# Two-operand work moved from GpSimd to VectorE, and an experts' activation taken by one ScalarE function from PSUM

## The chip, the cores and the metric

The kernel runs on one core of a Trainium2 chip. The core has TensorE (PE in the profile: matmuls, with weight loads listed as PEld), VectorE (DVE), ScalarE (ACT), GpSimd (POOL) and SyncE (SP), which here only issues transfers; 16 DMA engines move data. The metric is device microseconds (us) of one execution, lower is better. Everything is computed in f32 or better: a matrix product is made of three matmuls on a high and a low part of each operand (`hi` = the rounded operand, `lo` = operand − `hi`), so that for each tile loaded from memory somebody has to compute a copy `hi` and a difference `lo`.

## What is computed

Two layers run on 512 tokens of width 1024 (an mLSTM with dilated attention, then differential attention with RWKV). The end of the last layer, and the only place that the change touches, is a feed-forward part with 16384 experts of which each token uses 8 heads x 16:

```
q    = (xc @ peer_wq).reshape(C, 8, 2, 128)
s    = einsum('chpd,hpkd->chpk', q, peer_keys)
sv, si = top_k(s, 16)
cand = sv[..., 0, :, None] + sv[..., 1, None, :]
top_s, pos = top_k(cand.reshape(C, 8, 256), 16)
eidx = 128 * si[..., 0, a] + si[..., 1, b]          # a, b from pos
gate = softmax(top_s)
act  = gelu(einsum('chkd,cd->chk', peer_u[eidx], xc))
out  = einsum('chk,chkd->cd', gate * act, peer_v[eidx])
```

## The kernel before

`peer` (lines 2205 to 2417) does that part, after some 3100 us of the other layers. The 512 tokens are four blocks of 128. The first three (ND = 3) go a dense way: u·h is computed for all 128 blocks of 128 experts, each result multiplied by a dense gate matrix that is zero where a token did not choose an expert, and v is summed over all blocks. The fourth block fetches its chosen rows of u and v by indirect transfers on GpSimd (`gathered`).

**Routing.** Four steps g = 0 to 3 project the tokens with a quarter of `peer_wq` each. `wtile` (line 250) loads a 128x512 piece, ScalarE copies `whi`, and line 259 computes `wlo`, in turn on VectorE and GpSimd as long as `wboth` is true and on GpSimd alone afterwards (it goes false after the first half of g = 0). `route` takes the top 16s on VectorE (lines 2421 to 2425), and `experts` (after g = 1 and 3) turns positions into expert numbers: line 2476 compares (`eq`, VectorE), line 2477 multiplies by `sf` (GpSimd), line 2480 sums (VectorE).

**Building the gate matrix.** `gate_matrix` does 16 groups of 8 tokens for each of the three token blocks. A group makes four one-hot tiles of 128x1024 f16 from `iota` and the transposed numbers `tr`: `hot[0]`, `hot[1]` by comparing (lines 2521, 2522), `hot[2]`, `hot[3]` by multiplying `hot[0]` (lines 2523, 2524); `hot[3]` goes to GpSimd in every other group. 16 matmuls (line 2529 on) multiply the one-hots into the PSUM banks `acc0` to `acc3`, ScalarE copies each bank into `stage`, and each 32 tokens SP writes a `stage` to the table `wg` in DRAM (line 2536).

**Early blocks.** Between these, `early` (line 2279) computes u·h for NA = 34 of the 128 expert blocks, woven in by fixed counts (A0 = 40 steps before the building, AE = 24 in each token block, the rest behind): load a 128x1024 row block `raw` (line 2274), copy `uh` (ScalarE, line 2277), difference `ul` (line 2278, on GpSimd), 24 matmuls (lines 264 to 266), a copy `x` from PSUM (ScalarE, line 2293); six of the `x` stay, the others go to DRAM (`xd`). The first loads, copies and differences of these blocks carry a raised priority (HE), so the scheduler issues them well ahead, with three buffers of `uh`, `ul`. The scheduler (Tile) sets each engine's order from its own estimates; each engine then works strictly in that order and waits by semaphores.

**The main loop** (`for i in range(-7, P)`, written out in its order by `Core`, whose operations all carry line 62) does one expert block per iteration, with stages of several iterations at once: load v (512 KB), from i = 29 on also u (512 KB) and its 24 matmuls; the slice of the gate table, `W`, each fourth iteration; the activation of block i + 4 and i + 3; its product with `W` (`x<-x,W`); the parts `ah` (ScalarE) and `al` (VectorE) of that product; the parts of v (`v<-raw,v` on VectorE); and 18 matmuls of 512 columns into `acc`. The activation is the tanh form of gelu in four operations on 128x384 f32: Square (ScalarE), `gq<-gq,x` (VectorE), Tanh (ScalarE), `x<-gq,x` (VectorE), less a factor 0.5 that sits in the scale of the gate matrix. Up to i = 38 each iteration also takes one step of the fourth block's route on VectorE, afterwards its gathered rows.

Of the kernel before, what the change touches and what calls it, by code (L numbers as in the profile page):

```python
# [10 lines left out]
F32 = mybir.dt.float32  # L11
# [4 lines left out]
AF = mybir.ActivationFunctionType  # L16
ALU = mybir.AluOpType
AX = mybir.AxisListType
PSUM = bass.MemoryType.PSUM
P = 128  # L20
# [188 lines left out]
class Net:  # L209
# [40 lines left out]
    def wtile(self, w, r0, c0, n):  # L250

        nc = self.nc
        raw = self.wraw.tile([P, T], F32, tag="wraw", name=self.uid("wraw"))
        nc.sync.dma_start(raw[:, :n], w[r0:r0 + P, c0:c0 + n])
        hi = self.wsp.tile([P, T], F32R, tag="whi", name=self.uid("whi"))
        lo = self.wsp.tile([P, T], F32R, tag="wlo", name=self.uid("wlo"))
        nc.scalar.copy(hi[:, :n], raw[:, :n])
        self.wodd = not self.wodd
        (nc.vector if self.wodd and self.wboth else nc.gpsimd).tensor_tensor(lo[:, :n], raw[:, :n], hi[:, :n].bitcast(F32), op=ALU.subtract)
        return hi, lo  # L260

    def mm3(self, ps, lh, ll, rh, rl, first, last):
# [1942 lines left out]
    def peer(self, out):  # L2205

        nc, tc, a, c = self.nc, self.tc, self.a, self.c
        ND = NT - 1
        with ExitStack() as st:
# [71 lines left out]
            def early():  # L2281

                for i in [*range(NK, NA), *range(NK)]:
                    with tc.high_priority(HE):
                        uh, ul = split(a["ut"][i], "u", nc.gpsimd)
                    ps = ups.tile([P, T], F32, tag="u", name=self.uid("u"))[:, :n]
                    for k in range(KD):
                        b = slice(k * P, (k + 1) * P)
                        self.mm3(ps, uh[:, b], ul[:, b], hh[:, k, :n], hl[:, k, :n], k == 0, k == KD - 1)
                        if k % 2 and k < KD - 1:  # L2290
                            yield
                    x = xt()
                    nc.scalar.copy(x, ps)
                    if i < NK:
                        q["x", i] = x
                    else:
                        nc.sync.dma_start(xd[i], x)
                    yield
# [35 lines left out]
            for i in range(-7, P):  # L2334
# [22 lines left out]

                g = i + 3
                if 0 <= g < P:
                    x, h = q["x", g], q.pop(("h", g))  # L2360
                    k.scalar.activation(h, h, AF.Tanh, scale=0.044715 * math.sqrt(2.0 / math.pi))
                    k.vector.scalar_tensor_tensor(x, h, 1.0, x, op0=ALU.add, op1=ALU.mult)
                    k.vector.tensor_tensor(x, x, q["W", g // 4 * 4][:, :, g % 4], op=ALU.mult)
                g = i + 4
                if 0 <= g < P:
                    if g >= NA:
                        q["x", g] = xt()
                        k.scalar.copy(q["x", g], q.pop(("ps", g)))
                    x, h = q["x", g], gt("gq")
                    q["h", g] = h  # L2370
                    k.scalar.activation(h, x, AF.Square)
                    k.vector.scalar_tensor_tensor(h, h, 1.0 / 0.044715, x, op0=ALU.add, op1=ALU.mult)
                if 0 <= i + 1 < P:
                    x = q.pop(("x", i + 1))
                    ah, al = q["a", i + 1] = gt("ah", 2, F32R), gt("al", 2, F32R)
# [81 lines left out]
    def experts(self, g, dst, rt, nc):  # L2457
# [16 lines left out]
        for j, x in enumerate((a, b)):  # L2474
            eq = eqs[j] = rt.tile(sh, F16, tag="eq", name=self.uid("eq"), bufs=2)
            nc.vector.tensor_tensor(eq, x[:, :, None, :].to_broadcast(sh), self.i16[:, None].to_broadcast(sh), op=ALU.is_equal)
            nc.gpsimd.tensor_tensor(eq, eq, sf[:, j:8:2, :, None].to_broadcast(sh), op=ALU.mult)
        for j, eq in eqs.items():
            yield
            nc.vector.tensor_reduce(out=dst[1 + j][:, 2 * g - 2:2 * g + 2], in_=eq.rearrange("p h j k -> p h k j"), op=ALU.add, axis=AX.X)  # L2480
# [16 lines left out]
    def gate_matrix(self, t, gate, part, wg, bank, bp, iota):  # L2497
# [14 lines left out]
        for c0 in range(0, P, CH):  # L2512
            stage = bp.tile([P, P // 4, CH, 4], F32, tag="stage", name=self.uid("stage"), bufs=2)
            for q in range(0, CH, B):
# [6 lines left out]
                nc.vector.tensor_tensor(hot[0], iota[:, None].to_broadcast(sh), bc(0), op=ALU.is_equal)  # L2521
                nc.vector.tensor_tensor(hot[1], iota[:, None].to_broadcast(sh), bc(1), op=ALU.is_equal)  # L2522
                nc.vector.tensor_tensor(hot[2], hot[0], bc(2), op=ALU.mult)  # L2523
                (nc.gpsimd if n.start % 16 else nc.vector).tensor_tensor(hot[3], hot[0], bc(3), op=ALU.mult)  # L2524
                for e in range(B):
                    if e % 4 == 0:
                        ps = bank(f"acc{n.start // 4 % 2 * 2 + e // 4}")
# [2 lines left out]
                    nc.tensor.matmul(o, of(1, e), of(3, e), start=False, stop=True)  # L2530
                    if e % 4 == 3:
                        nc.scalar.activation(stage[:, :, q + e - 3:q + e + 1].rearrange("p g t e -> p t g e"),
                                             ps.rearrange("p (t g e) -> p t g e", t=4, e=4), AF.Copy, scale=0.5 / 1024)
                yield
            n = t * P + c0
            nc.sync.dma_start(wg[:, :, n:n + CH].rearrange("g j t e -> j g (t e)"), stage.rearrange("p g t e -> p g (t e)"))

    def gelu(self, x, tl, out=None):

        nc = self.nc  # L2540
        q = tl(list(x.shape), "gq")
        nc.scalar.activation(q, x, AF.Square)
        nc.vector.scalar_tensor_tensor(q, q, 1.0 / 0.044715, x, op0=ALU.add, op1=ALU.mult)
        nc.scalar.activation(q, q, AF.Tanh, scale=0.044715 * math.sqrt(2.0 / math.pi))
        out = q if out is None else out
        nc.vector.scalar_tensor_tensor(out, q, 1.0, x, op0=ALU.add, op1=ALU.mult)
        return out

    def gathered(self, t, h, gate, ei, out, gp, m5, row, Xd):

# [32 lines left out]
                yield  # L2583
        while held:
            step(None, None, dot)
        q = self.gelu(act, tl)
        nc.vector.scalar_tensor_tensor(q, q, 0.5, gate, op0=ALU.mult, op1=ALU.mult)
        yield
        for k in range(P):
            step(a["peer_v_2"][0], k, add)  # L2590
# [65 lines left out]
```

## Time and profile before

| | us |
|---|---|
| three runs | 4447.52, 4453.7, 4455.69 |
| median | 4453.7 |
| profiled execution, its own time | 4451.97 |
| its span in the profile | 4450.2 |

| engine | busy us | share of the span |
|---|---|---|
| TensorE | 4139.1 | 93% |
| VectorE | 3076.5 | 69% |
| ScalarE | 1979.0 | 44% |
| GpSimd | 1698.1 | 38% |

The shares are means over stages with different limits. For the change only the last 1350 us matter, and they are read by stage: the routing (3100 to 3263 us), the building of the gate matrix (3263, the first one-hot, to 3446, the last), the hand-over to the main loop (to 3482.5, its first matmul into `acc`), the loop's iterations without u matmuls (i = 0 to 28, to 3633.6), those with them (to 4402), and the tail. A duration in the profile is one instruction's; where instructions of an engine overlap slightly, the distance from start to start is what one costs.

### The profile page before, as it was taken

The page shows a single profiled execution, that of the slowest core. Times are in us where ns is not written, and L with a number is a line of the kernel's source. Part 1 is how long each engine was busy: PE and PEld are TensorE (multiplying, and loading weights), DVE is VectorE, ACT ScalarE, POOL GpSimd, SP SyncE. Part 2 cuts the span into 40 slices and gives each one's busy share as a digit, 9 for nine tenths or more (in the row PEclk, how much of TensorE's full clock was granted, in tenths as well). Part 3 has the DMA queues.
Part 4 walks back from the last instruction along what each step waited for, and adds up shares of the span by engine and source line. Part 5 has one row for each costly group of instructions (what it writes and reads, how often), then busy time and mean ns, then how long its engine had stood idle before and what let it go on. Part 6 is the DMA issues. An engine that isn't in the chain of part 4 may idle for free. (4 is left out here: it accounts for less than half of the span.)

```text
span 4450.2 us, 83415 instructions
## 1 busy us (share of the span) xinstructions
PE 4139.1 (93%) x32239; PEld 3601.2 (81%) x32239; DVE 3076.5 (69%) x5903; ACT 1979.0 (44%) x4240; POOL 1698.1 (38%) x1501
## 2 busy tenths in 40 slices
PE   7999999899999899989999999998877889999998
PEld 6889998788888788767777777777767779999997
DVE  4665224565565665546776676646999797999999
ACT  3544234355323445435555555534234444444443
POOL 3324444333444343322333333425355102445443
PEclk8999999899999999989999999999988999999999
DMA  4325334333556421110000001265256657999997
GB/s 138 79 58 164 93 96 129 88 77 97 162 173 201 132 75 55 49 33 20 29 29 26 29 27 42 75 194 186 71 164 196 197 173 269 339 348 338 334 339 258
DMA packets 437062, 621.08 MB, mean 140 GB/s; under 512 B 32868, under 2 KB 318708, under 8 KB 436536
## 3 DMA queue, kind: packets, MB, share of 16 engines
q1 hardware_dynamic: 393464, 472.17, 33.8%
q0 software_dynamic: 36864, 134.23, 8.5%
q10 hardware_dynamic: 6336, 9.35, 0.7%
q8 instruction: 253, 4.15, 0.4%
q14 instruction: 145, 1.19, 0.1%
HBM read 549.36 MB, written 48.24 MB: 134 GB/s over the span
## 5 line engine op out<-in xcount | busy, mean ns | idle before, releaser
L62 POOL TENSOR_TENSOR wlo<-wraw,whi 128x512 fp32r<-128x512 f32 x451 | 613.5, 1367 | 883.9 <-ACT whi L62 840.7
L62 ACT CAST whi<-wraw 128x512 fp32r<-128x512 f32 x572 | 347.4, 617 | 555.2 <-PE mm L62 369.1
L62 PE MATMUL acc<-v,ah 128*128 128x512 f32 x1536 | 417.7, 394 | 4.3 <-ACT ah L62 4.3
L62 PE MATMUL u<-hph,u 128*128 128x384 f32 x1504 | 398.8, 336 | 0.0
L62 PE MATMUL mm<-whi,u 128*128 128x256 f32 x2048 | 376.8, 285 | 4.9 <-ACT u L62 1.9
L62 PE MATMUL mm<-xh,whi 128*128 128x512 f32 (+2 forms) x880 | 341.2, 388 | 8.1 <-ACT r L62 5.1
L1497 POOL TENSOR_TENSOR wbl<-wblk,wbh 128x256 fp32r<-128x256 f32 (+1 forms) x184 | 149.4, 812 | 510.8 <-ACT wbh L1496 349.5
L62 PEld LDWEIGHTS acc<-v,ah 128*128 128x128 f32 x1536 | 291.5, 191 | 60.0 <-ACT ah L62 4.6
L62 PEld LDWEIGHTS mm<-whi,u 128*128 128x128 f32 x2048 | 323.0, 193 | 6.9 <-ACT u L62 2.5
L62 PE MATMUL mm<-xh,wlo 128*128 128x512 f32 (+2 forms) x880 | 328.0, 373 | 0.0
L62 PE MATMUL mm<-xl,whi 128*128 128x512 f32 (+2 forms) x880 | 328.0, 373 | 0.0
L62 PE MATMUL mm<-wlo,u 128*128 128x256 f32 x1024 | 291.5, 285 | 5.1 <-POOL wlo L62 4.6
L62 PEld LDWEIGHTS u<-hph,u 128*128 128x128 f32 x1504 | 273.1, 188 | 3.7
L62 PE MATMUL acc<-v,al 128*128 128x512 f32 x768 | 242.7, 398 | 28.7 <-DVE al L62 28.6
L2557 POOL DMA_INDIRECT gr<-in_peer_u_dram,ei x128 | 165.1, 1290 | 251.6 <-DVE act L2571 158.3
L62 PE MATMUL u<-hpl,u 128*128 128x384 f32 x752 | 252.7, 336 | 0.0
L2557 POOL DMA_INDIRECT gr<-in_peer_v_dram,ei x128 | 170.0, 1328 | 183.4 <-DVE pr L2578 152.8
L62 PE MATMUL mm<-whi,xh 128*128 128x256 f32 x768 | 237.5, 309 | 0.0
L62 PE MATMUL mm<-whi,xl 128*128 128x256 f32 x768 | 220.7, 287 | 1.0 <-POOL xl L62 1.0
L62 PE MATMUL mm<-wlo,xh 128*128 128x256 f32 x768 | 220.2, 287 | 0.0
L62 DVE TENSOR_TENSOR wlo<-wraw,whi 128x512 fp32r<-128x512 f32 x121 | 102.5, 847 | 147.2 <-ACT whi L62 141.5
L62 PEld LDWEIGHTS mm<-wlo,u 128*128 128x128 f32 x1024 | 197.7, 193 | 6.6 <-POOL wlo L62 5.4
(598 smaller groups left out, 11734.3 us busy)
## 6 DMA issues: line engine op xcount, KB each, us to landing
raw<-in_ut_dram SPq DMA_DIRECT2D x128, 512.0 KB
raw<-in_peer_v_dram SPq DMA_DIRECT2D x128, 512.0 KB
wraw<-in_w_in_dram SPq DMA_DIRECT2D x184, 256.0 KB
wraw<-in_w_down_dram SPq DMA_DIRECT2D x160, 256.0 KB
wraw<-in_w_up_dram SPq DMA_DIRECT2D x152, 256.0 KB
mraw<-in_w_mod_dram SPq DMA_DIRECT2D x96, 256.0 KB
wg<-stage SPq DMA_DIRECT2D x12, 2048.0 KB
W<-wg SPq DMA_DIRECT2D x32, 768.0 KB
```

Of the source, the lines that this page charges most:

```text
L62: return lambda *a, **k: self.tc.keep_in_program_order(f(*a, **k))
L1497: (nc.vector if self.wn > WN and n % 2 else nc.gpsimd).tensor_tensor(lo, raw, hi.bitcast(F32), op=ALU.subtract)
L2557: tc.keep_in_program_order(nc.gpsimd.indirect_dma_start(out=r, out_offset=None, in_=w, in_offset=bass.IndirectOffsetOnAxis(ap=ei[:, i:i + ...
```

## The change

Three things change.

1. The differences and products that GpSimd did in `peer` with two operand tiles go to VectorE: `wlo` at line 259 once `wboth` is false, `ul` of the early blocks (line 2278), the product of `eq` with `sf` (line 2477), and `hot[3]` (line 2524). GpSimd keeps the indirect transfers.
2. The activation becomes one ScalarE instruction, the tanh-form gelu function, and reads PSUM in the place of the copy that was there: in `early` the `x` that is stored is already activated; in the loop Square, Tanh and the two VectorE operations are gone, and for blocks from 34 on the copy from PSUM is the activation. The function includes the factor 0.5, so the gate matrix is scaled by 1/1024 and not by 0.5/1024.
3. The gathered block's activation is one function too, and one product on VectorE in place of three operations.

```diff
-        (nc.vector if self.wodd and self.wboth else nc.gpsimd).tensor_tensor(lo[:, :n], ...)
+        (nc.vector if self.wodd or not self.wboth else nc.gpsimd).tensor_tensor(lo[:, :n], ...)
...
-                        uh, ul = split(a["ut"][i], "u", nc.gpsimd)
+                        uh, ul = split(a["ut"][i], "u", nc.vector)
...
-                    nc.scalar.copy(x, ps)
+                    nc.scalar.activation(x, ps, AF.Gelu_apprx_tanh)
...
-                    x, h = q["x", g], q.pop(("h", g))
-                    k.scalar.activation(h, h, AF.Tanh, scale=0.044715 * math.sqrt(2.0 / math.pi))
-                    k.vector.scalar_tensor_tensor(x, h, 1.0, x, op0=ALU.add, op1=ALU.mult)
+                    x = q["x", g]
                     k.vector.tensor_tensor(x, x, q["W", g // 4 * 4][:, :, g % 4], op=ALU.mult)
...
-                        k.scalar.copy(q["x", g], q.pop(("ps", g)))
-                    x, h = q["x", g], gt("gq")
-                    q["h", g] = h
-                    k.scalar.activation(h, x, AF.Square)
-                    k.vector.scalar_tensor_tensor(h, h, 1.0 / 0.044715, x, op0=ALU.add, op1=ALU.mult)
+                        k.scalar.activation(q["x", g], q.pop(("ps", g)), AF.Gelu_apprx_tanh)
...
-            nc.gpsimd.tensor_tensor(eq, eq, sf[:, j:8:2, :, None].to_broadcast(sh), op=ALU.mult)
+            nc.vector.tensor_tensor(eq, eq, sf[:, j:8:2, :, None].to_broadcast(sh), op=ALU.mult)
...
-                (nc.gpsimd if n.start % 16 else nc.vector).tensor_tensor(hot[3], hot[0], bc(3), op=ALU.mult)
+                nc.vector.tensor_tensor(hot[3], hot[0], bc(3), op=ALU.mult)
...
-                                             ps.rearrange("p (t g e) -> p t g e", t=4, e=4), AF.Copy, scale=0.5 / 1024)
+                                             ps.rearrange("p (t g e) -> p t g e", t=4, e=4), AF.Copy, scale=1.0 / 1024)
...
-        q = self.gelu(act, tl)
-        nc.vector.scalar_tensor_tensor(q, q, 0.5, gate, op0=ALU.mult, op1=ALU.mult)
+        q = tl([P, P], "gq")
+        nc.scalar.activation(q, act, AF.Gelu_apprx_tanh)
+        nc.vector.tensor_tensor(q, q, gate, op=ALU.mult)
```

Everything up to the routing stays as it was. From there on the scheduler orders anew, and the lines of `gate_matrix` and `experts` are numbered six lower. The functions of the activation and of the softmax's exponential do not lie in one table of ScalarE: nine table loads are added, seven of them before the loop (between line 2485, the exponential, and line 2293) and two in the loop at i = 38.

VectorE while the gate matrix is built, before. `hot_N<-iota` are the comparisons, `hot_N<-hot_M` the products, `tr` belongs to a token block:

```order
L2521 TENSOR_TENSOR hot_41828<-iota_40510,tr_41004 128x1024
L2521 TENSOR_TENSOR hot_41865<-iota_40510,tr_41004 128x1024
L2522 TENSOR_TENSOR hot_41829<-iota_40510,tr_41004 128x1024
L2523 TENSOR_TENSOR hot_41830<-hot_41828,tr_41004 128x1024
L2524 TENSOR_TENSOR hot_41831<-hot_41828,tr_41004 128x1024
L2521 TENSOR_TENSOR hot_41914<-iota_40510,tr_41004 128x1024
L2521 TENSOR_TENSOR hot_41948<-iota_40510,tr_41004 128x1024
L2522 TENSOR_TENSOR hot_41866<-iota_40510,tr_41004 128x1024
L2523 TENSOR_TENSOR hot_41867<-hot_41865,tr_41004 128x1024
```

The same place on VectorE after the change:

```order
L2515 TENSOR_TENSOR hot_41702<-iota_40510,tr_40926 128x1024
L2516 TENSOR_TENSOR hot_41703<-iota_40510,tr_40926 128x1024
L2517 TENSOR_TENSOR hot_41704<-hot_41702,tr_40926 128x1024
L2518 TENSOR_TENSOR hot_41705<-hot_41702,tr_40926 128x1024
L2278 TENSOR_TENSOR u_41988<-raw_41985,u_41987 128x1024
L2515 TENSOR_TENSOR hot_41747<-iota_40510,tr_41004 128x1024
```

Every group has its four one-hots on VectorE, and the difference of an early block stands in the same queue behind every second or third group.

VectorE at the end of the routing's step g = 2, before (`iota` is the building's table, `cd` and `ts` are the second top 16):

```order
L2446 TENSOR_TENSOR cd_40293<-sv_40270 128x2x16
L2449 TENSOR_TENSOR cd_40293<-sv_40270 128x2x24
L2443 CAST sf_40268<-si_40271 128x64
L2449 TENSOR_TENSOR cd_40293<-sv_40270 128x2x48
L2302 CAST iota_40510<-tables_39092 128x256
L2421 MAX ts_39105<-cd_40293 128x8 x2
```

The same place after:

```order
L2417 MATCH_REPLACE cd_40293<-ts_39105,cd_40293 128x88 x2
L2418 MAX ts_39105<-cd_40293 128x8 x2
L2419 MAX_INDEX ps_40269<-ts_39105,cd_40293 128x8 x2
L2278 TENSOR_TENSOR u_40685<-raw_40682,u_40684 128x1024
L259 TENSOR_TENSOR wlo_40423<-wraw_40420,whi_40422 128x512
L259 TENSOR_TENSOR wlo_40441<-wraw_40438,whi_40440 128x512
L2278 TENSOR_TENSOR u_40719<-raw_40716,u_40718 128x1024
L2302 CAST iota_40510<-tables_39092 128x256
L2415 MAX sv_40852<-S_40307 128x8
```

The last two `wlo` of the projection g = 3 now stand behind the whole route of g = 2, and right ahead of the route of g = 3 (`S_40307`), which reads that projection.

VectorE in the loop's iterations without u matmuls, before:

```order
L62 SCALAR_TENSOR_TENSOR gq_43629<-gq_43629,x_43533 128x384
L62 TENSOR_TENSOR al_43633<-x_43410,ah_43632 128x384
L62 TENSOR_TENSOR v_43637<-raw_43531,v_43636 128x1024
L62 MAX sv_43615<-S_39098 128x8
L62 MAX_INDEX si_43616<-sv_43615,S_39098 128x8
L62 MATCH_REPLACE S_39098<-sv_43615,S_39098 128x128
L62 MAX sv_43615<-S_39098 128x8
L62 MAX_INDEX si_43616<-sv_43615,S_39098 128x8
L62 SCALAR_TENSOR_TENSOR x_43533<-gq_43629,x_43533 128x384
L62 TENSOR_TENSOR x_43533<-x_43533,W_43408 128x384
```

The same place after:

```order
L62 TENSOR_TENSOR x_43454<-x_43454,W_43380 128x384
L62 TENSOR_TENSOR al_43575<-x_43382,ah_43574 128x384
L62 TENSOR_TENSOR v_43579<-raw_43488,v_43578 128x1024
L62 MAX sv_43562<-S_39098 128x8
L62 MAX_INDEX si_43563<-sv_43562,S_39098 128x8
L62 MATCH_REPLACE S_39098<-sv_43562,S_39098 128x128
L62 MAX sv_43562<-S_39098 128x8
L62 MAX_INDEX si_43563<-sv_43562,S_39098 128x8
L62 TENSOR_TENSOR x_43490<-x_43490,W_43380 128x384
```

The two SCALAR_TENSOR_TENSOR of an iteration are gone, and nothing else of it has moved.

## Rows read from the trace of the kernel before

**Rows 1.** Busy time by stage; columns: us, then PE, PEld, DVE, ACT, POOL, PEclk, DMA, GB/s:

```profile
3100.00:3263.00 163.00, 132.96 (x698) 119.76 (x697) 156.45 (x708) 46.67 (x98) 77.10 (x46) 0.91 0.29 90
3263.00:3446.30 183.30, 139.54 (x1148) 125.80 (x1148) 180.42 (x171) 75.09 (x134) 105.68 (x42) 0.89 0.64 194
3446.30:3482.50 36.20, 31.88 (x203) 31.24 (x201) 5.74 (x9) 15.18 (x27) 12.02 (x5) 0.97 0.70 227
3482.50:3633.60 151.10, 130.32 (x522) 100.37 (x523) 146.64 (x365) 69.42 (x119) 5.24 (x2) 0.96 0.55 173
3633.60:4402.00 768.40, 768.21 (x3913) 702.40 (x3912) 735.82 (x956) 357.64 (x559) 332.32 (x252) 1.00 0.90 322
```

**Rows 2.** Timeline of VectorE in the building; columns: start, duration, operation:

```profile
3423.93 2.86 DVE L2523 TENSOR_TENSOR hot<-hot,tr 128x1024 f16<-128x1024 f16 x1
...
3429.62 0.68 DVE L2523 TENSOR_TENSOR hot<-hot,tr 128x1024 f16<-128x1024 f16 x1
3430.22 0.68 DVE L2522 TENSOR_TENSOR hot<-iota,tr 128x1024 f16<-128x1024 f16 x1
```

**Rows 3.** Timeline of GpSimd in the same stretch; in brackets its idle time before:

```profile
3423.64 2.60 POOL L2278 TENSOR_TENSOR u<-raw,u 128x1024 fp32r<-128x1024 f32 x1 [1.50 <-ACT u L2277]
...
3435.01 1.98 POOL L2524 TENSOR_TENSOR hot<-hot,tr 128x1024 f16<-128x1024 f16 x1 [6.47 <-PE acc L2530]
```

**Rows 4.** Groups of GpSimd, 3100 to 3482 us: busy, mean ns | idle before, releaser:

```profile
L2278 POOL TENSOR_TENSOR u<-raw,u 128x1024 fp32r<-128x1024 f32 x34 | 87.1, 2568 | 66.7 <-ACT u L2277 66.6
L2524 POOL TENSOR_TENSOR hot<-hot,tr 128x1024 f16<-128x1024 f16 x24 | 57.8, 2410 | 51.2 <-PE acc L2530 31.1 <-DVE hot L2521 20.1
L259 POOL TENSOR_TENSOR wlo<-wraw,whi 128x512 fp32r<-128x512 f32 x22 | 28.1, 1296 | 19.0 <-ACT whi L257 19.0
L2477 POOL TENSOR_TENSOR eq<-eq,sf 128x1024 f16<-128x1024 f16 x12 | 23.0, 1916 | 41.8 <-DVE pb L2469 32.2 <-DVE eq L2476 9.6
```

**Rows 5.** Stage of the building, instructions on `hot` alone; columns: us, PE, PEld, DVE, POOL:

```profile
3263.00:3446.30 183.30, 57.93 (x736) 47.13 (x736) 177.90 (x168) 57.84 (x24) 0.89 0.64 194
```

**Rows 6.** Groups of VectorE, 3100 to 3482 us:

```profile
L2470 DVE TENSOR_SCALAR pz<-pa 128x64 f32<-128x64 f16 x6 | 11.6, 1936 | 0.0
L2443 DVE CAST sf<-si 128x64 f16<-128x64 uint32 x12 | 6.7, 557 | 0.0
...
L2467 DVE SCALAR_TENSOR_TENSOR pb<-pa,ps 128x64 f16<-128x64 f16 x6 | 1.3, 213 | 0.0
```

**Rows 7.** VectorE's differences, tiles `u` and `wlo`: ns least/median/most, first and last start:

```profile
L62 DVE TENSOR_TENSOR u<-raw,u x94: 1206/1217/1232, 3631.5 to 4397.6; 128x1024 fp32r<-128x1024 f32 x94
...
L259 DVE TENSOR_TENSOR wlo<-wraw,whi x6: 674/680/1381, 3053.9 to 3071.7; 128x512 fp32r<-128x512 f32 x6
```

**Rows 8.** Timeline of VectorE in an iteration of the loop's first stage:

```profile
3501.01 0.54 DVE L62 SCALAR_TENSOR_TENSOR x<-gq,x 128x384 f32<-128x384 f32 x1
3501.58 0.85 DVE L62 TENSOR_TENSOR x<-x,W 128x384 f32<-128x384 f32 x1
3502.34 0.56 DVE L62 SCALAR_TENSOR_TENSOR gq<-gq,x 128x384 f32<-128x384 f32 x1
3502.81 0.56 DVE L62 TENSOR_TENSOR al<-x,ah 128x384 fp32r<-128x384 f32 x1
```

**Rows 9.** Pieces of the chain that ended last: start, duration, instructions:

```profile
3650.94 4.17 PE u L62 x24
3655.11 4.08 PE acc L62 x18
```

**Rows 10.** Timeline of SP's queue at the hand-over:

```profile
3451.76 0.37 SPq L2536 DMA_DIRECT2D wg<-stage  x1
...
3461.27 0.79 SPq L2344 DMA_DIRECT2D W<-wg  x2
```

**Rows 11.** Timeline of PE in the tail:

```profile
4419.52 0.73 PE L62 MATMUL acc<-v,al 128*128 128x512 f32 x2 [2.87 <-DVE al L62]
```

**Rows 12.** ScalarE's table loads in the whole kernel: busy, mean ns | idle before:

```profile
L62 ACT ACT_TABLE_LOAD x4 | 5.1, 1283 | 0.1
```

More of the change, by code (lines that the diff above doesn't have):

```diff
@@ L258, in wtile @@
         self.wodd = not self.wodd
-        (nc.vector if self.wodd and self.wboth else nc.gpsimd).tensor_tensor(lo[:, :n], raw[:, :n], hi[:, :n].bitcast(F32), op=ALU.subtract)
+        (nc.vector if self.wodd or not self.wboth else nc.gpsimd).tensor_tensor(lo[:, :n], raw[:, :n], hi[:, :n].bitcast(F32), op=ALU.subtract)
         return hi, lo
@@ L2536, in gate_matrix @@
             nc.sync.dma_start(wg[:, :, n:n + CH].rearrange("g j t e -> j g (t e)"), stage.rearrange("p g t e -> p g (t e)"))
[L2538 to L2547, printed above, removed]
     def gathered(self, t, h, gate, ei, out, gp, m5, row, Xd):
```

## The prediction

> **What bounds the kernel now.** I read the busy time by stage first, because the change touches only what lies behind 3100 us [rows 1]. In the building VectorE is busy 180.4 of 183.3 us, TensorE 139.5; in the loop's first stage VectorE 146.6 of 151.1, TensorE 130.3; then, with u matmuls, TensorE 768.2 of 768.4. So VectorE is the bound up to 3633.6 us, but for the hand-over, and TensorE from there on. Whatever the change gives must come from the first three stages and the tail; the stage of 768 us can give nothing.
>
> Next, why VectorE is full in the building. Its timeline beside GpSimd's is what to see: a one-hot that took 2.86 us began at 3423.93, while GpSimd computed a two-operand difference from 3423.64 to 3426.24; at 3429.62 the same operation took 0.68 us, and the next began 0.60 later [rows 2]. GpSimd had nothing then: its instruction at 3435.01 has 6.47 us of idle time before it, back to 3428.5 [rows 3]. So VectorE waits inside its instruction until GpSimd's ends. The whole stage says the same: 168 one-hots take 177.9 us, 1.06 each [rows 5], against 0.60 undisturbed.
>
> **Part 1, the building: what it removes.** Four kinds of GpSimd instruction leave: 34 differences of u, 24 one-hots, 22 `wlo`, 12 products, 196.0 us together [rows 4]. With them the blocking goes. The 168 one-hots at 0.60 would be 100.8, so 77.1 less [rows 2, 5]. `pz` at 1.936 us and `sf` at 0.557 are small operations beside one of the same shape at 0.213; 6 x 1.72 = 10.3 and 12 x 0.34 = 4.1 [rows 6]. That is 91.5 us off VectorE.
>
> **What it adds.** All of it to VectorE's queue: 34 differences of u at 1.22, the loop's own price for that operation, 41.5; 22 `wlo` at 0.68, 15.0 [rows 7]; 24 one-hots and 12 products of the same size and type at 0.60, 14.4 and 7.2 [rows 2]. Together 78.1. Net VectorE gains 91.5 - 78.1 = 13.4 us between 3100 us and the last one-hot.
>
> In detail it moves the load between stages: routing gets all `wlo` and products and, by the order, some ten of the u differences, and grows; the building then has 192 one-hots at 0.60 (115) and some 24 differences (29), 144 us in place of 180, close to TensorE's 139.5. There two things can eat into the gain. The order puts the last two `wlo` of the projection g = 3 behind the whole route of g = 2, so the scores that the next route reads come later; at the worst VectorE idles while the 24 matmuls of 512 columns that read these two run (18 such take 4.08 [rows 9], so 5.4) and the scores are copied: by estimate up to 7 us. And each u difference now waits in VectorE's queue for ScalarE's copy, with one-hots behind it. On the other side smaller operations that I didn't price (`pb`, `ei`, `cd`) also lose their blocking. I set these against each other and keep 13.4, with 0 to 35 as bounds.
>
> The upper bound is TensorE itself: 139.5 + 31.9 of the 219.5 us up to the first matmul into `acc`.
>
> **Table loads.** Nine are added; one takes 1.283 us [rows 12], 11.5 together, on an engine busy 75 of 183 us [rows 1]. Three pairs lie at exponentials while VectorE still routes other token blocks; only the last can delay the first one-hot, by 2.6 at most. I take 0. The Trainium skill, "ScalarE: Activation LUTs", section What ACT_TABLE_LOAD costs, adds a drain and gives about 2.66 us per switch; by that the nine would be 24 us and the bound for the last pair 5.3, still beside VectorE's work. The trace has the load's 1.283 and shows no drain.
>
> **Part 2, the hand-over.** From the last one-hot to the first matmul into `acc` 36.2 us pass [rows 1]. Two things end late there. SP writes the last `stage` at 3451.76 and fetches the first `W` at 3461.27 [rows 10], and the product and its split must follow; and TensorE still has 6.5 early blocks at 4.17 [rows 9] to do, 27 us. By the new order 2.75 of them stand behind the last one-hot, 11.5 us. The write and fetch remain: 5.5 from the last one-hot to the write, 9.5 to the fetch, and by estimate some 9 for the transfer and the product. 36.2 becomes about 24: 12 less, with bounds 0 and 17. These early blocks go to where TensorE had gaps, in the building, which is the cover; if TensorE gets behind there, this gain goes back.
>
> **Part 3, the loop without u matmuls.** An iteration loses two VectorE operations. From start to start `x<-gq,x` costs 0.57 and `gq` 0.47 [rows 8], 1.04 together, 30.2 in 29 iterations. VectorE falls from 146.6 to 116.4. TensorE becomes next: 18 matmuls are 4.08 [rows 9], 29 x 4.08 = 118.3. The two are as good as equal, so some waiting remains; I take the floor and the 4.5 us that VectorE idled before: 123, 28 less. Bounds: 33 (the floor) and 15 (half, if transfers or the chain over `ah` and `al` set the pace; the DMA engines are at 0.55 here against 0.90 in the next stage, which speaks against it). ScalarE loses two operations and a copy's place is taken by the function; at 69 of 151 us its price doesn't matter.
>
> **Part 4, the rest.** From 3633.6 on an iteration is 4.17 + 4.08 on TensorE: 0. VectorE, at 735.8 of 768.4 us, is nearly late there, and is late in the tail: TensorE waits four times for `al`, 0.83 to 2.87 us, 7.7 together; the longest is shown [rows 11]. With 1.04 us less per iteration VectorE has slack, and I take 7 of it, bounds 3 and 8. The gathered block's activation is one instruction once: nothing.
>
> **Sum.** 13.4 + 12 + 28 + 7 = 60.4 us. The profiled execution took 4451.97, so 4391.6; the median of the runs lies 1.7 higher, 4393.3. I predict 4393.
>
> **Rivals.**
> *The building doesn't get shorter (4419).* VectorE gains 36 us there, but TensorE, its matmuls interleaved with one-hots by fixed counts, is at a granted clock of 0.89 and hardly below VectorE's new load; routing grows by as much as the building shrinks, or the late scores take it. Then only loop and tail count, 28 + 7: 4418.7. For it: 144 against 139.5. Against: the hand-over's blocks have to be done some time, and TensorE had 44 us of gaps.
> *TensorE-bound throughout (4365).* VectorE's waits vanish: 219.5 - 171.4 = 48 up to `acc`, 33 in the loop, 8 in the tail, 89 together: 4365. For it: the unpriced small operations, and the blocking of 91.5 all gone. Against: 139.5 is the sum, and one-hots and matmuls must alternate.
> *Slower: the waits go into VectorE's queue (4479).* GpSimd's queue stood waiting for ScalarE's copies 66.6 us before u differences and 19.0 before `wlo` [rows 4]. On an idle engine that costs nothing. In VectorE's queue each such wait holds up the one-hots behind it, and through them the matmuls and the `stage`. All 85.6 us of it would end at 4453.7 - 60.4 + 85.6 = 4479; from 60.4 of 85.6, some 70%, the change loses. For it: the order shows each u difference straight ahead of one-hots. Against: the loads and copies have raised priority and three buffers, and ScalarE is at 41% in the building, so most of the waits were of an engine ahead of its need.
> *The change doesn't do it (4485).* If the one-hots stay at 1.06 us because something other than GpSimd slows them, 91.5 us of the sum are missing: 4453.7 + 31.1 = 4485. Against: the pairs of rows at 3423.9 and 3429.6.
> The Trainium skill, "Perfetto Trace Analysis", section Optimizing Scalar/DVE Operations, speaks for this side: with a saturated VectorE it suggests to move work to ScalarE or even GpSimd, the reverse of this change, and by that alone the 78.1 us would be added where VectorE is full. The same passage warns that the two share a read port, so that moving between them may not help; rows 2 and 3 agree with the warning, 2.86 against 0.68 us.
>
> **How the numbers follow.** Chances: the forecast, 4375 to 4410, 0.63; building unchanged 0.16; TensorE-bound 0.10; waits in VectorE's queue 0.08 (0.03 of it so partial that nothing is measured); no effect on the one-hots 0.03. The range 4362 to 4430 takes in the forecast and the two cases beside it. Below 0.2%, about 9 us, a measurement of this kernel can't tell a difference from none. Faster: 0.63 + 0.16 + 0.10 = 0.89; same 0.03; slower 0.08.
>
> **What would show it.** One-hots of 0.68 us throughout, and VectorE near 145 us in a building of about 150; routing longer than 163; the loop's first stage near 123 with TensorE above 95%; the stage from i = 29 at 768; no waits for `al` in the tail. I am wrong where VectorE's rows before a u difference or a `wlo` show idle time released by ScalarE, where one-hots keep durations above 1 us, or where the first `W` product waits on a late `wg` as long as now.

## The result, and the profile after

The changed kernel takes 4370.19 us (median of four runs, 4367.73 to 4373.44) against 4451.76 of the kernel before (four runs, 4447.52 to 4455.69): a ratio of 0.9821, with a 95% interval of 0.9809 to 0.9833. That is 81.6 us less where 60.4 were forecast; 4393 was predicted, in a range from 4362 to 4430. The direction, the places and the mechanism held; three of the four terms were too small and the fourth a little too large, and the largest miss is in the building. The time lies in the range, but below the band of 4375 to 4410 to which the forecast itself gave a chance of 0.63.

The profiled execution took 4373.44 us, 78.5 less than that of before. Its busy time by stage, cut at the same events as [rows 1]: the first and the last one-hot, the first matmul into `acc`, the first u matmul, and close to the last one. Columns: us, then PE, PEld, DVE, ACT, POOL, granted clock, DMA share, GB/s.

```profile
3100.00:3254.00 154.00, 137.80 (x743) 123.88 (x742) 142.46 (x653) 54.49 (x105) 0.00 (x0) 0.97 0.33 101
3254.00:3423.20 169.20, 141.98 (x1234) 124.79 (x1233) 166.97 (x327) 83.79 (x145) 0.00 (x0) 0.91 0.72 226
3423.20:3441.50 18.30, 12.90 (x84) 12.42 (x83) 2.69 (x3) 5.03 (x10) 0.00 (x0) 0.91 0.77 244
3441.50:3566.50 125.00, 123.04 (x522) 99.22 (x523) 119.80 (x319) 46.48 (x62) 0.00 (x0) 0.97 0.67 214
3566.50:4333.20 766.70, 766.70 (x3907) 701.29 (x3906) 658.07 (x770) 275.55 (x375) 333.64 (x255) 1.00 0.90 325
4333.20:4371.70 38.50, 29.50 (x135) 24.49 (x133) 27.88 (x29) 7.04 (x10) 7.83 (x6) 0.94 0.36 131
```

| up to | before | after | gain | forecast |
|---|---|---|---|---|
| last one-hot | 3446.3 | 3423.2 | 23.1 | 13.4 |
| first matmul into `acc` | 36.2 | 18.3 | 17.9 | 12 |
| first u matmul of the loop | 151.1 | 125.0 | 26.1 | 28 |
| end | 816.6 | 805.2 | 11.4 | 7 |

By these cuts two of the prediction's signs look missed: the routing got shorter and not longer than 163 us, and the building lasts 169 and not 150. That comes from one one-hot, at 3254.0, which stands alone in VectorE's order; the next begins at 3271.2. From there the building is 152.0 us long, and the routing before it 171.2:

```profile
3271.20:3423.20 152.00, 133.00 (x1189) 117.26 (x1190) 149.85 (x254) 76.69 (x134) 0.00 (x0) 0.92 0.77 241
```

GpSimd does nothing between 3100 and 3566 us. VectorE is still full in the building, 167 of 169 us; what it does there got cheaper, as its groups between 3100 and 3480 us show (busy us, mean ns | idle before, releaser):

```profile
L2278 DVE TENSOR_TENSOR u<-raw,u 128x1024 fp32r<-128x1024 f32 x34 | 41.3, 1216 | 2.7 <-ACT u L2277 2.7
L2518 DVE TENSOR_TENSOR hot<-hot,tr 128x1024 f16<-128x1024 f16 x48 | 32.8, 682 | 0.0
...
L259 DVE TENSOR_TENSOR wlo<-wraw,whi 128x512 fp32r<-128x512 f32 x22 | 14.6, 684 | 2.7 <-ACT whi L257 2.7
L2471 DVE TENSOR_TENSOR eq<-eq,sf 128x1024 f16<-128x1024 f16 x12 | 14.6, 1214 | 0.0
...
L62 DVE TENSOR_TENSOR x<-x,W 128x384 f32<-128x384 f32 x12 | 10.0, 841 | 15.0 <-DMA W<-wg 15.0
...
L2437 DVE CAST sf<-si 128x64 f16<-128x64 uint32 x12 | 2.3, 188 | 0.0
...
L2464 DVE TENSOR_SCALAR pz<-pa 128x64 f32<-128x64 f16 x6 | 1.1, 185 | 0.0
```

Here the forecast can be checked operation by operation. All four kinds of one-hot stand at 0.682 us. `pz` fell from 1.936 to 0.185 and `sf` from 0.557 to 0.188 [rows 6]. The differences of u cost 1.216 and `wlo` 0.684, as taken from [rows 7]. Two readings differ from it: the product of `eq` with `sf` costs 1.214 and not 0.60, and in the two moved differences VectorE waited 2.7 us each for ScalarE, together 5.4, where GpSimd had waited 85.6 [rows 4].

The hand-over on SP's queue, to set beside [rows 10]:

```profile
3425.45 0.39 SPq L2530 DMA_DIRECT2D wg<-stage  x1
3435.50 0.80 SPq L2344 DMA_DIRECT2D W<-wg  x2
```

The last `stage` is written 2.3 us behind the last one-hot, `W` is fetched 10.0 later, and VectorE's first product follows at 3440.0 after 15.0 us in which it had nothing but this to wait for (the row `x<-x,W` above). TensorE's early blocks ended at 3436. So the way over `wg` is now what bounds the hand-over. Before, VectorE waited there for the activation of the early blocks, which TensorE was still computing, and its first product, at 3475.6, didn't wait for `W`:

```profile
3470.83 0.56 DVE L62 SCALAR_TENSOR_TENSOR gq<-gq,x 128x384 f32<-128x384 f32 x1 [24.58 <-ACT gq L62]
```

In the tail one wait for `al` is left of the four at [rows 11]:

```profile
4356.11 0.73 PE L62 MATMUL acc<-v,al 128*128 128x512 f32 x2 [0.97 <-DVE al L62]
```

### The profile page after: what moved, and what is told of

It is laid out like the page before. It is cut to its first block, busy times and chain, and to the rows that moved or that the text cites. A ratio compares the mean times of both kernels' runs of the same rounds, so it can differ in the third digit from the quotient of the medians.

```text
span 4371.7 us, 82968 instructions
## 1 busy us (share of the span) xinstructions
PE 4116.9 (94%) x32239; PEld 3584.3 (82%) x32239; DVE 2930.0 (67%) x5743; ACT 1876.6 (43%) x3992; POOL 1489.0 (34%) x1403
## 5 line engine op out<-in xcount | busy, mean ns | idle before, releaser
L62 ACT CAST ah<-x 128x384 fp32r<-128x384 f32 x128 | 65.8, 514 | 379.7 <-PE acc L62 368.6
```

The lines of the kernel that those rows point to most:

```text
L62: return lambda *a, **k: self.tc.keep_in_program_order(f(*a, **k))
```

## The experiments

All times are medians; ratios are to the kernel before on the same chip, with their intervals. The changed kernel's is 0.9821 (0.9809 to 0.9833).

### One half of the change at a time

The first kernel keeps the activation by one function and gives GpSimd its instructions back:

```diff
-        (nc.vector if self.wodd or not self.wboth else nc.gpsimd).tensor_tensor(lo[:, :n], ...)
+        (nc.vector if self.wodd and self.wboth else nc.gpsimd).tensor_tensor(lo[:, :n], ...)
-                        uh, ul = split(a["ut"][i], "u", nc.vector)
+                        uh, ul = split(a["ut"][i], "u", nc.gpsimd)
-            nc.vector.tensor_tensor(eq, eq, sf[...], op=ALU.mult)
+            nc.gpsimd.tensor_tensor(eq, eq, sf[...], op=ALU.mult)
-                nc.vector.tensor_tensor(hot[3], hot[0], bc(3), op=ALU.mult)
+                (nc.gpsimd if n.start % 16 else nc.vector).tensor_tensor(hot[3], hot[0], bc(3), op=ALU.mult)
```

> The changed kernel with its four kinds of two-operand instructions back on GpSimd; the activation stays one ScalarE function. Theory (two independent gains): routing, building and hand-over as before the change, first matmul into acc near 3482, loop's first stage 125 us, no waits for al in the tail: 37 us off the kernel before, about 4415. Rival (the gain of 23 and 18 us in building and hand-over comes from the new order and from the shorter chain to the first product, not from GpSimd's leaving): first matmul into acc near 3450 to 3465, 4385 to 4400.

Measured: 4414.18, ratio 0.9913 (0.9897 to 0.993), 37 us less than before. Its execution with a profile was the longest of its four (4427.97), and its first matmul into `acc` came at 3496. The one-hots alone (PE, PEld, DVE, POOL), in a stretch that starts where the building of before starts (its own first one-hot comes at 3283.3), and the loop's first stage:

```profile
3263.00:3462.30 199.30, 56.88 (x736) 46.31 (x736) 173.88 (x168) 63.20 (x24) 0.88 0.60 183
```

```profile
3496.30:3621.40 125.10, 121.81 (x524) 98.78 (x525) 120.47 (x317) 46.82 (x62) 4.79 (x2) 0.99 0.67 214
```

The one-hots are as slow as before (1.03 us each, against 1.06 at [rows 5]), the hand-over is 34 us long, and the loop's first stage has its whole gain. The new activation gives nothing ahead of `acc`: the 26 us of the loop and some 12 behind it (804.8 us from the first u matmul to the end, against 816.6) account for the 37.

The second is the kernel before with the same four lines edited the other way, the activation left in four operations.

> The kernel before with the four kinds of two-operand instructions moved to VectorE, activation still in four operations. Theory: building and hand-over as after the change (last one-hot 3423, first matmul into acc 3441), loop's first stage again 151 us, tail again 45: 41 us off, about 4411. Rival (the gains are one: with VectorE full in the loop the earlier start is lost there): 4425 to 4450.

Measured: 4408.32, ratio 0.9900 (0.9883 to 0.9916), 42.9 us less. The one-hots of line 2521 in the whole run, and the loop's first stage:

```profile
L2521 DVE TENSOR_TENSOR hot<-iota,tr x48: 671/677/684, 3250.2 to 3417.2; 128x1024 f16<-128x1024 f16 x48
```

```profile
3441.60:3592.20 150.60, 129.35 (x523) 99.69 (x524) 146.03 (x368) 69.53 (x119) 0.00 (x0) 0.97 0.56 175
```

The first matmul into `acc` comes at 3441.6, as after the change, and the loop's first stage is at 150.6 as before it. 37.0 + 42.9 = 79.9 of the change's 81.6: within the noise the two halves add, and neither needs the other.

### Back to GpSimd, one kind at a time

In each of these three runs the scheduler also gives VectorE another order (in the first, the one-hot that stood alone at 3254.0 is gone and the first comes at 3276.0). Their times hold that too; what the engines do to each other is read from the rows.

```diff
-                        uh, ul = split(a["ut"][i], "u", nc.vector)
+                        uh, ul = split(a["ut"][i], "u", nc.gpsimd)
```

> The changed kernel with only the 34 differences of u in the early blocks back on GpSimd. VectorE loses 34 x 1.14 = 39 us of work. Theory (GpSimd's instruction blocks VectorE's): one-hots of 2.4 to 2.9 us beside each, 1.6 us lost for each of some 24 in the building and less in the routing, so 5 to 15 slower than the change: 4375 to 4385. Rival (no blocking, VectorE's load is what counts): 15 to 30 faster than the change, 4340 to 4355.

Measured: 4423.1, ratio 0.9937 (0.9921 to 0.9954): 53 us slower than the change, where 5 to 15 were expected. The rival is out, but the theory had the size wrong, and for a reason. Here are VectorE, then GpSimd at the same time, then GpSimd's differences in the whole run (ns least/median/most), then two sums of waits (us, how often, the longest):

```profile
3359.33 0.68 DVE L2516 TENSOR_TENSOR hot<-iota,tr 128x1024 f16<-128x1024 f16 x1
...
3375.59 0.68 DVE L2515 TENSOR_TENSOR hot<-iota,tr 128x1024 f16<-128x1024 f16 x1
3381.40 2.25 DVE L2516 TENSOR_TENSOR hot<-iota,tr 128x1024 f16<-128x1024 f16 x1 [5.14 <-PE acc L2524]
```

```profile
3360.23 18.23 POOL L2278 TENSOR_TENSOR u<-raw,u 128x1024 fp32r<-128x1024 f32 x1 [7.40 <-ACT u L2277]
```

```profile
L2278 POOL TENSOR_TENSOR u<-raw,u x34: 2338/2404/23294, 3111.7 to 3474.4; 128x1024 fp32r<-128x1024 f32 x34
```

```profile
DVE hot L2516 <- PE acc L2524: 40.9, 9, 8.2
...
PE u L266 <- POOL u L2278: 19.2, 3, 8.1
```

From 3359.3 to 3376.3 VectorE issues one-hots 0.60 us apart without a break, 28 of them, each at 0.68: it isn't blocked at all. GpSimd, whose instruction began at 3360.2, is: the difference, 2.4 us at the median, takes 18.2 and ends at 3378.5, 2.2 behind VectorE's last one-hot. Three others take 23.3, 21.6 and 13.2 us in the same way. Here GpSimd gets in only when VectorE has to wait for TensorE. TensorE in its order waits for such differences (three waits of 19.2 us together), meanwhile the one-hots' tiles stay occupied, and VectorE waits for TensorE in its turn: nine waits, 40.9 us, which is most of the 53. So the exclusion works both ways, and a VectorE that runs instructions back to back keeps GpSimd out for a whole run. What was expected, 1.6 us per GpSimd instruction on VectorE, is the other half of it.

```diff
-                nc.vector.tensor_tensor(hot[3], hot[0], bc(3), op=ALU.mult)
+                (nc.gpsimd if n.start % 16 else nc.vector).tensor_tensor(hot[3], hot[0], bc(3), op=ALU.mult)
```

> The changed kernel with only 24 of the 192 one-hots (hot[3] of every other group) back on GpSimd. Theory: VectorE loses 14 us of work and 24 x 1.6 = 38 to blocking, so up to 24 slower, 4380 to 4394. Rival (no blocking): up to 14 faster, 4356 to 4368.

Measured: 4407.47, ratio 0.9905 (0.9888 to 0.9921): 37 slower than the change, where 24 were expected at most, and with the same signs in the trace. GpSimd's one-hots in the run, and the waits they cause:

```profile
L2518 POOL TENSOR_TENSOR hot<-hot,tr x24: 1887/2346/9272, 3277.1 to 3448.8; 128x1024 f16<-128x1024 f16 x24
```

```profile
PE acc L2524 <- POOL hot L2518: 30.4, 7, 5.5
```

A one-hot of 2.35 us takes up to 9.27, and TensorE waits for them seven times, 30.4 us together. Taking 14 us of work from a full VectorE made the kernel 37 slower.

```diff
-        (nc.vector if self.wodd or not self.wboth else nc.gpsimd).tensor_tensor(lo[:, :n], ...)
+        (nc.vector if self.wodd and self.wboth else nc.gpsimd).tensor_tensor(lo[:, :n], ...)
```

> The changed kernel with only the 22 differences wlo of the projection back on GpSimd (all of them lie in the routing, ahead of the building). Theory as it stands after the runs with u and hot (a GpSimd read and a VectorE instruction with two operands exclude each other, and who comes second waits, GpSimd through whole runs of VectorE): routing VectorE is less dense in such instructions, so little is lost: 0 to 12 slower than the change, 4370 to 4382. Rival (the in-order place of wlo in VectorE's queue delays the scores of the projection g = 3): 5 to 10 faster, 4360 to 4365.

Measured: 4363.75 (4355.86 to 4369.79), ratio 0.9806 (0.9789 to 0.9822). The interval overlaps the change's, so whether these 22 are better on GpSimd stays open, and theory and rival with it; the ends of the two intervals leave out a loss of more than some 6 us. That they don't lose as the other two kinds do fits their place in the routing, where VectorE does many operations on one tile between those on two; that this is the reason isn't shown.

### GpSimd's instruction without any data that anyone needs

The runs so far change who waits for whose data. These three don't: in each of the 48 groups GpSimd writes a tile that nobody reads, by one of the three instructions below. In the routing and the building VectorE's instructions stand in the order of the changed kernel, but for two near the end that move by a few places, so these runs can be compared with it instruction by instruction.

```diff
                 nc.vector.tensor_tensor(hot[3], hot[0], bc(3), op=ALU.mult)
+                dd = bp.tile(sh, F16, tag="dd", name=self.uid("dd"), bufs=1)
+                nc.gpsimd.tensor_tensor(dd, iota[:, None].to_broadcast(sh), bc(3), op=ALU.mult)   # first run
+                nc.gpsimd.tensor_copy(dd, iota[:, None].to_broadcast(sh))                         # second
+                nc.gpsimd.memset(dd, 0.0)                                                         # third
```

> The changed kernel with one added GpSimd instruction per group of the building, 48 in all: a product of iota with tr (128x1024 f16, two operands read from SBUF) into a tile that nobody reads. No data hangs on it. Theory (blocking inside the instruction, without any wait for data): one-hots of 2 us and more while it runs, 48 x 1.6 = 77 us longer building, 4410 to 4450. Rival (VectorE was held up by waits for GpSimd's results and buffers): one-hots stay at 0.68, time as the change, 4370.

Measured: 4437.14, ratio 0.9973 (0.9961 to 0.9984), 67 us slower than the change. The added instructions, and VectorE's one-hots during the second batch of them:

```profile
L2520 POOL TENSOR_TENSOR dd<-iota,tr x48: 1893/2220/4068, 3259.9 to 3368.7; 128x1024 f16<-128x1024 f16 x48
```

```profile
3334.05 2.38 DVE L2516 TENSOR_TENSOR hot<-iota,tr 128x1024 f16<-128x1024 f16 x1
3336.35 2.38 DVE L2517 TENSOR_TENSOR hot<-hot,tr 128x1024 f16<-128x1024 f16 x1
3338.65 2.38 DVE L2518 TENSOR_TENSOR hot<-hot,tr 128x1024 f16<-128x1024 f16 x1
```

While GpSimd works, a one-hot costs 2.38 us, one for each of its instructions. 67 us for 48 is 1.4 each, with no data in play. They ran early and together, not spread over the groups. While they run, from 3260 to 3371 us, VectorE's instructions fall 67 us further behind those of the changed kernel, and after that hardly any more.

> As the run before, but the added instruction is a copy with one operand (iota, 128x1024 f16). If any read by GpSimd blocks VectorE's two-operand instructions: as the run before, in proportion to GpSimd's duration. If only a two-operand instruction does: 4370, one-hots at 0.68.

Measured: 4392.33, ratio 0.9870 (0.9853 to 0.9886), 22 slower. The copies, and a small VectorE operation on two tiles among them (between 3190 and 3260 us) that takes 0.216 us undisturbed:

```profile
L2520 POOL COPY dd<-iota x48: 1035/1043/2051, 3224.2 to 3286.1; 128x1024 f16<-128x1024 f16 x48
```

```profile
L2463 DVE SCALAR_TENSOR_TENSOR pb<-pz,pb 128x64 f16<-128x64 f32 x1 | 1.1, 1053 | 0.0
```

It takes as long as a copy. So one operand is enough, and the longer instruction costs more: 0.46 us per copy of 1.04, 1.4 per product of 2.2. These copies had ended, at 3287, before most one-hots began, which then stand at 0.69; VectorE falls 21 us behind the changed kernel while they run, and no further.

> As the run before, but the added instruction is a memset of the same tile, which reads nothing. Theory (the shared thing is a read): no effect, 4370, one-hots at 0.68. Rival (any GpSimd instruction that touches SBUF blocks): 4400 and more.

Measured: 4376.5 (4367.06 to 4379.19), ratio 0.9833 (0.9815 to 0.9852), which can't be told from the change. The memsets, and two of VectorE's operations on one tile between 3190 and 3260 us, where they ran:

```profile
L2520 POOL MEMSET dd<- x48: 952/952/977, 3201.1 to 3248.5; 128x1024 f16 x48
```

```profile
L2459 DVE TENSOR_SCALAR pa<-r 128x64 f16<-128x64 uint32 x1 | 1.0, 974 | 0.0
L2437 DVE CAST sf<-si 128x64 f16<-128x64 uint32 x5 | 1.3, 267 | 0.0
```

Nearly as long as the copies, but VectorE's operations on two tiles aren't touched: the u differences stand at 1.214 in that stretch, where the copies had raised them to 1.415, and `pb`, 1.053 beside the copies, at 0.214. Some operations on one tile are: without the memsets `pa` takes 0.186 there and `sf` 0.189. There are few of them, and VectorE falls only 1 us behind. The Trainium skill, "SBUF — State Buffer", section Who interferes with whom, has this as a rule: a VectorE instruction with two inputs in SBUF contends with a GpSimd instruction that reads SBUF, not with one that only writes it. For operations on two tiles the three runs agree: 1.4 us each for the product, 0.46 for the copy, nothing for the memset. The operations on one tile, like `pa` here and `pz` before the change, are slowed too, and that sentence doesn't cover them.

### The loop's first stage

```diff
                     x = q["x", g]
+                    if 0 <= i < 29:
+                        for _ in range(2):
+                            k.vector.scalar_tensor_tensor(gt("gq"), x, 1.0, x, op0=ALU.add, op1=ALU.mult)
                     k.vector.tensor_tensor(x, x, q["W", g // 4 * 4][:, :, g % 4], op=ALU.mult)
```

> The changed kernel with two operations added on VectorE in the loop's iterations 0 to 28 (128x384 f32, of the same form as those removed, result unused); ScalarE's chain stays short. Theory (the loop's first stage gained because VectorE has 1.04 us less per iteration): first stage back at 148 to 152 us, about 4395. Rival (it gained because the chain Square, product, Tanh, product is gone): stays at 125 to 130, 4370 to 4375.

Measured: 4397.75, ratio 0.9884 (0.9868 to 0.9901), 27.6 slower than the change. Its first stage:

```profile
3440.90:3592.40 151.50, 132.14 (x523) 101.41 (x524) 146.96 (x368) 46.92 (x62) 0.00 (x0) 0.95 0.54 174
```

151.5 us, with VectorE at 147.0 as before the change, though ScalarE keeps its short chain (46.9 us busy). So the stage gained by VectorE's smaller load and not by the shorter chain. After the change TensorE, busy 123.0 of the 125.0 us, is as near to bounding it as VectorE.

### The table loads

```diff
-        nc.scalar.activation(ts, ts, AF.Exp)
+        nc.scalar.activation(ts, ts, AF.Square)
```

> The changed kernel with Square in the place of the exponential in the softmax of the chosen experts (the gates are thereby other numbers), which takes away eight of the added table loads. Theory (ScalarE has room, the loads are beside other work): 4367 to 4373, as the change. Rival (each load with what lies around it stands ahead of a one-hot or a stage): 8 x 1.28 = 10 or more faster, below 4360.

Measured: 4372.62 (4362.73 to 4382.78), ratio 0.9833 (0.9810 to 0.9856): no different from the change, though the executions scatter more. Eight loads fewer bring nothing that can be seen, and the interval leaves out the rival's 10 us.

### A version that goes further

After the change TensorE has gaps in the building (142 of 169 us), and each early block that is put there leaves the stage in which TensorE is the bound.

```diff
-NA = 34
+NA = 40
-A0, AE = 40, 24
+A0, AE = 40, 32
```

> The changed kernel with 40 in place of 34 early blocks (24 in place of 18 of them woven into the building). Theory (since the change TensorE has 27 us of gaps in the building and VectorE has to do only 1.14 us more per block): six iterations of the loop cost 4.3 us and not 8.25, 24 less, and the building gets 7 to 17 longer: 4353 to 4363. Rival (the building is as full on TensorE as on VectorE): nothing gained, 4368 to 4375.

Measured: 4362.76, ratio 0.9810 (0.9794 to 0.9827), at most a little faster than the change. Its building and its hand-over:

```profile
3254.00:3430.40 176.40, 155.15 (x1325) 137.50 (x1324) 173.54 (x336) 91.11 (x154) 0.00 (x0) 0.92 0.72 233
3430.40:3456.40 26.00, 24.08 (x149) 23.60 (x147) 5.88 (x7) 8.32 (x14) 0.00 (x0) 1.00 0.74 246
```

The building got 7 us longer, as expected. The hand-over went from 18.3 to 26.0 and TensorE is busy in 24.1 of it: blocks that found no room ahead of the last one-hot. From the first matmul into `acc` to the end the run takes 906.5 us, against 930.2 of the changed kernel: the 24 expected, and most of it is lost again ahead of `acc`. The last run, against this one, moves two blocks ahead of the building and gives `wlo` back to GpSimd:

```diff
-A0, AE = 40, 32
+A0, AE = 48, 32
-        (nc.vector if self.wodd or not self.wboth else nc.gpsimd).tensor_tensor(lo[:, :n], ...)
+        (nc.vector if self.wodd and self.wboth else nc.gpsimd).tensor_tensor(lo[:, :n], ...)
```

> The run with 40 early blocks again, with two differences: 48 in place of 40 steps of early blocks lie ahead of the building and as many fewer behind the last one-hot, and the 22 wlo are computed on GpSimd. Theory (in the run with 40 early blocks the hand-over rose from 18 to 26 us, because TensorE had six blocks behind the last one-hot; those ahead of the building find room): hand-over back at 18 to 20 us, 4349 to 4358, faster than both kernels. Rival (TensorE's gaps are set by the alternation with one-hots, so blocks can't be put into them): 4360 to 4366, as that run.

Measured: 4345.99 (five runs, 4345.82 to 4354.01), ratio 0.9761 (0.9748 to 0.9775): faster than both kernels, by 24 us than the changed one. Its execution with a profile was the longest of the five; from it the stretch from 3254 us to the last one-hot, and the hand-over:

```profile
3254.00:3427.20 173.20, 166.50 (x1401) 149.90 (x1402) 172.04 (x304) 93.98 (x162) 0.00 (x0) 0.98 0.79 246
3427.20:3444.40 17.20, 15.28 (x97) 14.96 (x96) 3.25 (x4) 5.39 (x10) 0.00 (x0) 1.00 0.87 296
```

The hand-over is back at 17.2 us, about what was expected. TensorE is now at 96% in the building, at a granted clock of 0.98 where it was 0.91. Which of the two edits brought how much wasn't separated, and with `wlo` gone from its queue VectorE has another order as well.

## Why the prediction was right, and where its sizes were off

**What bounds the kernel** held: nothing came from the stage with u matmuls, where TensorE is as busy as before.

**Part 1** named the right cause. That GpSimd's instruction holds VectorE's, without any data between them, is shown by the added product that nobody reads (67 us). That VectorE would be full still, and near TensorE, held too (149.9 of 152.0 us). The size was too small, 13.4 against 23.1. VectorE's busy time up to the last one-hot fell by 27.4 us (156.5 + 180.4 to 142.5 + 167.0), and its idle time rose by 4.3. The step that failed is the one that set the unpriced small operations against the extra waits and kept zero. Before, some of them (same columns as [rows 6]):

```profile
L2449 DVE TENSOR_TENSOR cd<-sv 128x96 f32<-128x96 f32 x12 | 5.0, 417 | 0.0
L2446 DVE TENSOR_TENSOR cd<-sv 128x32 f32<-128x32 f32 x12 | 5.0, 414 | 0.0
...
L2471 DVE SCALAR_TENSOR_TENSOR pb<-pb,pz 128x64 f16<-128x64 f16 x6 | 4.7, 784 | 0.0
L2487 DVE SCALAR_TENSOR_TENSOR ei<-sel,sel 128x128 int32<-128x128 f32 x3 | 3.6, 1184 | 0.0
```

and after:

```profile
L2443 DVE TENSOR_TENSOR cd<-sv 128x96 f32<-128x96 f32 x12 | 3.0, 248 | 0.0
...
L2440 DVE TENSOR_TENSOR cd<-sv 128x32 f32<-128x32 f32 x12 | 2.1, 173 | 0.0
L2465 DVE SCALAR_TENSOR_TENSOR pb<-pb,pz 128x64 f16<-128x64 f16 x6 | 1.2, 208 | 0.0
...
L2481 DVE SCALAR_TENSOR_TENSOR ei<-sel,sel 128x128 int32<-128x128 f32 x3 | 0.8, 277 | 0.0
```

These four alone are 11.2 us, and they could have been priced by an undisturbed neighbour, as `pz` was. The other way, the products with `sf` were priced at a one-hot's 0.60 and cost 14.6 in place of 7.2. The operands have the same size and type; `sf` is spread along the innermost axis, where the one-hots' operands have two elements side by side, and that may be why, but no run tests it. The waits that were set against all this came to 5.4 us for the moved operations, and the late scores to a single wait of 3.5.

**Part 2**, 12 against 17.9, was too careful in the terms of the way over `wg`: 5.5 + 9.5 + 9 were taken, and 2.3 + 10.0 + 6.0 measured. The 9 was an estimate; and the 5.5 were taken over from the kernel before, where TensorE's last matmuls on one-hots began 5.2 us behind the last one-hot and now 1.8. That TensorE's blocks would find room ahead of the last one-hot held: TensorE is busy 12.9 us in the hand-over, and was 31.9.

**Part 3**, 28 against 26.1: VectorE's load was nearly right (119.8 measured, 116.4 forecast); the stage ended 6.7 us above TensorE's floor of 118.3, and not 4.5, with TensorE busy for 123.0 of the 125.0. The run with two operations added on VectorE gives the whole gain back.

**Part 4**, 7 against 11.4. Three of the four waits are gone. Behind the two longest waits before, TensorE's matmuls also ran slower for some us, which the sum left out: behind the one of 2.87 four of them took 1.85 us, where four take 1.07 elsewhere, and the granted clock from 4420 to 4423 us was 0.52, near the lower of its two levels. The second run, with the old activation, still has waits of 1.61, 2.83 and 2.10 us there; the first has the gain.

**The table loads** were taken at 0; the run without eight of them agrees. By the Trainium skill's figure ("ScalarE: Activation LUTs", What ACT_TABLE_LOAD costs) these eight would be an estimated 21 us of ScalarE's time. The rows of after show 1.283 us each and no drain (the next activation starts 0.01 us behind a load where it has nothing else to wait for), and nothing of either came out in the time.

**The rivals.** The waits did not go into VectorE's queue: 5.4 of 85.6 us. That the building doesn't get shorter, and that the one-hots stay slow, are out by the rows. Nearest in the end was the rival in which TensorE bounds everything, 4365, which had a chance of 0.10: building and hand-over gave 41 of the 48 us that it allowed, the first stage 26 of 33. It is near by the number and not by its mechanism, for VectorE is still full in the building, and TensorE has gaps there that the last run fills. The forecast was too cautious in the same direction at three places: the direction needed no luck, but that the time lies in the range, 8 us from its lower end, owes something to a width of 68 us. What the Trainium skill suggests for a full VectorE ("Perfetto Trace Analysis", Optimizing Scalar/DVE Operations), work given to GpSimd, was weighed in the prediction; two of the three runs that did so were 53 and 37 us slower, and the third, with `wlo`, can't be told from the change.

## What to carry to other kernels

A GpSimd instruction that reads SBUF is not free parallel work beside a VectorE that runs operations on two tiles back to back: read the same operation's duration with and without GpSimd busy, and price every VectorE group that is slower than its like, small ones too. Moving work from GpSimd to a full VectorE can pay, and taking a little of it back can cost more than it saves; where VectorE runs few operations on two tiles, as with `wlo` in the routing, it cost nothing that could be measured. After such a move look at the engine that has gaps now; filling TensorE's, with `wlo` back on GpSimd, gave another 24 us.

## What the runs showed of the hardware

- The exclusion is not shared out evenly. VectorE ran 27 two-operand instructions 0.60 us apart while one on GpSimd that needs 2.4 us didn't finish (18.2 us); the longest took 23.3 us. In the other order a one-hot of 0.68 took 2.38 for each GpSimd instruction of 2.2.
- One operand read by GpSimd is enough to hold up VectorE (a 128x64 operation on two tiles of 0.216 us took 1.05 beside copies of 1.04). A memset leaves the operations on two tiles alone (0.214) but not all on one tile: a 128x64 operation of 0.186 us took 0.974, as long as a memset, and a conversion 0.267 in place of 0.189.
- A product of 128x1024 f16 with one operand spread along its innermost axis took 1.214 us, the one-hots' products of the same size 0.682.
- The tanh-form gelu from PSUM costs ScalarE what the copy did: 0.492 us against 0.474 for 128x384 f32.
